# First stage of a convolution and SwiGLU block: low weights on GpSimd, all rows of the conditioning weights on VectorE, tile 0's scale and shift on two engines

## The chip, the cores and the metric

The kernel runs on one core of one Trainium2 chip. A core has TensorE (PE, matrix products into PSUM banks), VectorE (DVE), ScalarE (ACT), GpSimd (POOL), and SyncE (SP), whose queue issues most of the transfers. The metric is the device time of one execution in microseconds (us); lower is better.

## The reference

One layer of a diffusion trunk, with 1024 tokens of 1024 features in fp32. The first stage, which the change touches, computes `h` and the first products of `h @ w_in`:

```python
sh1, sc1, g1, sh2, sc2, g2 = split(silu(c) @ ada_w + ada_b, 6)
h = rmsnorm(x, norm1_g) * (1.0 + sc1) + sh1
gate_b, gate_c, hv = split(h @ conv_w_in, 3)
conv = conv3_grid(gate_c * hv, conv_w)
x = x + g1 * ((gate_b * conv) @ conv_w_out)
x = x + g2 * swiglu(modulate(rmsnorm(x, norm2_g), sh2, sc2), ffn_w_in, ffn_w_out)
out = rmsnorm(x, final_g)
```

## The kernel before

TensorE multiplies in a reduced fp32 format. To keep the precision, each operand is split into a high part (a cast) and a low part (raw minus high), and a product is made of three terms: high x high, low tokens x high weights, high tokens x low weights (TERMS). This holds in all stages. The long later stages (the rest of the convolution mixer by Strassen's scheme, then the SwiGLU) keep TensorE busy and aren't touched.

The first stage has the first 512 tokens and seven column blocks ("pairs", EARLY) of conv_w_in, which fill seven PSUM banks. It goes over the eight feature tiles k = 0 to 7 (128 features each, KD = 8, KH = 4). For each tile it does the following.

- Ada(k) makes tile k's shift and scale: the column sums of ada_w, weighted by silu(c). Its eight "rows" are blocks of 128 input features; each row is a tile of 128 x 256 (shift and scale beside each other). `sums` multiplies rows by their weights into two accumulators (row r goes to accumulator r modulo 2; rows 0 and 1 start them, the others add), `merge` adds the two, `total` sums over the partitions on TensorE, with one-column products in which the accumulators meet a column of ones. A number of rows ("direct") may be left to TensorE, which then multiplies them by the column of weights. `columns` turns the totals into a column of scale1 and one of shift1.
- `tokens(k)` calls `columns`, makes the high tokens (A11h or A12h, from xT, the normalized and transposed tokens) on ScalarE, and has the low weights w0l made (`low0`); `rows_ahead` then sums rows of the next tile.
- `tokens_low(k)` makes the modulated tokens in place (xT), their low part on VectorE (`low1`: A11l, A12l), the cast of the next tile's weights (`high0`: w0h), and the remaining rows of the next tile (`rows_left`, with `merge`).
- The 21 products of a tile go over the pairs term by term (`by_term`); `total_at` says ahead of which of them the next tile's total stands. Tiles 3 and 4 have an order of their own, because the seven banks are copied out half way (`save_p1`, tiles p).

The program's order is the order of the work on SP, DVE, ACT and PE in this stage (a block of manual scheduling); GpSimd's order is set by the scheduler. Loads run ahead by three tiles (`next_loads`). Before tile 0, four token tiles (Tokens) are loaded, normalized (ScalarE squares, GpSimd x_ms and x_r, VectorE scales), transposed by TensorE and copied to xT by ScalarE. `keep_busy` is a filler product on TensorE.

In tile 0 the token tile is modulated twice: A11h on ScalarE, and an unrounded copy h0 (tile h) on VectorE.

Of the kernel before, what the change touches and what calls it, by code (L numbers as in the profile page):

```python
# [11 lines left out]
AF = mybir.ActivationFunctionType  # L12
# [12 lines left out]
def trunk_kernel(ctx: ExitStack, tc: tile.TileContext, x, c, ada_w, ada_b, norm1_g, norm2_g,  # L25
                 conv_w_in, conv_w, conv_w_out, ffn_w_in, ffn_w_out, final_g, out):
    nc = tc.nc
# [18 lines left out]
    def f(ap):  # L46
        return ap.bitcast(F32)
# [16 lines left out]
    def t2(name, shape=None):  # L64
        return sb.tile(shape or [P, H], F32, name=name, tag="t2", bufs=6)
# [7 lines left out]
    def sub(o, a, b):  # L73
        return nc.vector.tensor_tensor(o, a, b, op=ALU.subtract)  # L74
# [67 lines left out]
    class Ada:  # L142
# [26 lines left out]
        def merge(self):  # L169
            add(self.acc[0], self.acc[0], self.acc.pop())  # L170

        def total(self, apart=False):
            self.ps = [bank(f"{self.name}_ps{j}") for j in range(2)] if apart else [ada_ps[0]] * 2
            rows = [(self.rows[r], cs[:, r:r + 1]) for r in range(KD - self.direct, KD)]
            sums = [(acc, ones) for acc in self.acc]
            n = len(rows) + len(sums)
            products = [(j, i, *part) for j in range(2) for i, part in enumerate(rows + sums)]
            if apart:
                products.sort(key=lambda p: p[1] >= len(rows))
            for j, i, part, by in products:  # L180
                nc.tensor.matmul(self.ps[j][:, j:j + 1], lhsT=part[:, j, :], rhs=by, start=i == 0, stop=i == n - 1)  # L181

        def columns(self):

            k = self.k
            nc.scalar.activation(scale1[:, k:k + 1], self.ps[1][:, 1:2], AF.Identity, scale=g1c[:, k:k + 1],
                                 bias=gab1[:, k:k + 1])
            nc.scalar.activation(shift1[:, k:k + 1], self.ps[0][:, 0:1], AF.Identity, bias=ab[:, k:k + 1])

    class AdaRow:  # L190

# [117 lines left out]
    def h_of(k, h):  # L309
        hi, lo = A[QUARTER[h, k // KH], k % KH // 2]  # L310
        return hi[:, k % 2, :], lo[:, k % 2, :]
# [7 lines left out]
            if h == 0:  # L319
                nc.scalar.copy(h_of(k, h)[0], o)  # L320

    def modulate1_both(k, raw=None):

        o, by, plus = xT[0][k // 2][:, k % 2, :], scale1[:, k:k + 1], shift1[:, k:k + 1]
        nc.scalar.activation(h_of(k, 0)[0], o, AF.Identity, scale=by, bias=plus)
        nc.vector.tensor_scalar(o if raw is None else raw, o, by, plus, op0=ALU.mult, op1=ALU.add)

    def low1(k, h):
        hi, lo = h_of(k, h)
        sub(lo, xT[h][k // 2][:, k % 2, :], f(hi))  # L330
# [29 lines left out]
        nc.scalar.copy(w0[k][0], w0raw[k])  # L360

    def low0(k):
        sub(w0[k][1], w0raw[k], f(w0[k][0]))

    def term0(k, pair, terms=range(3)):
        if pair not in xbank:
# [5 lines left out]

    p1_left = []

    def save_p1(pair, tile, later=False):
        nc.scalar.copy(tile, xbank[pair])
        if later:
            p1_left.append((pair, tile))
        else:
            nc.gpsimd.dma_start(aside[PAIRS.index(pair)], tile)  # L380
# [298 lines left out]

    with in_order(ENG.SP, ENG.DVE, ENG.Activation, ENG.PE):  # L680
        xs = [Tokens(t) for t in range(TH)]
        ada = [Ada(0, 2)]
        ada[0].load()
        ada[0].load()
        load0(0)
# [2 lines left out]
        def next_loads(k):  # L688

            if k < KD:  # L690
                ada.append(Ada(k, 2 if k == 1 else 0))
                ada[k].load()
                ada[k].load()
                load0(k)
            elif k == KD:
                xs.extend(Tokens(TH + i) for i in range(TH))
            elif k == KD + 1:
                more.extend(First(pair) for pair in LATER[:2])
                for m in more:
                    m.load(0)  # L700
            elif k == KD + 2:
                more.extend(First(pair) for pair in LATER[2:])
                for m in more[2:]:
                    m.load(0)
                for m in more:
                    m.load(1)
# [6 lines left out]
        for i in range(TH):  # L713
            if i == TH - 1:
                ada[0].sums(0, 1)
            xs[i].scale()
            for g in range(2):
                xs[i].transposes(g)
            xs[i].copies(*(range(KH) if i < TH - 1 else (0,)))
        high0(0)  # L720
        ada[0].sums(2, 3, 4, 5)
        ada[0].total(True)
        keep_busy(1)
        ada[0].columns()
        h0 = t2("h0")
        modulate1_both(0, h0)
        xs[TH - 1].copies(1, 2, 3)
        ada_ps.append(bank("ada_ps"))

        def rows_ahead(k):  # L730

            if k < KD:
                ada[k].sums(2, 3, 4)

        def rows_first(k):
            if k < KD:
                ada[k].sums(0, 1, scalar=True)

        def rows_left(k):
            if k < KD:  # L740
# [24 lines left out]
        def saved(k, n, pair):  # L765
            if k == KH - 1:
                if n % 2 == 0:
                    kept[n // 2] = t_s(f"p1_{n}", [P, 2, H])
                save_p1(pair, kept[n // 2][:, n % 2, :], later=True)

        by_term = [(pair, (i,)) for i in range(3) for pair in EARLY]
        by_half = by_term[:7] + [(pair, (1, 2)) for pair in EARLY]
        first_five, first_four = [[(pair, (i,)) for i in range(3) for pair in EARLY[:n]] +
                                  [(pair, range(3)) for pair in EARLY[n:]] for n in (5, 4)]
        orders = [by_term] * (KH - 1) + [first_five, first_four] + [by_term] * (KH - 2) + [by_half]
        total_at = [14] * (KH - 1) + [11, 12] + [14] * (KH - 1)
        sub(h_of(0, 0)[1], h0, f(h_of(0, 0)[0]))
        rows_first(1)
        tokens(0)
        tokens_low(0)  # L780
        for k in range(KD):
            if k:
                next_loads(k + 3)
            if k + 3 == KD + 2:
                store_p1()
            last = k == KD - 1
            if k == 6:
                nc.vector.tensor_copy(xT[0][0][:, 0, :], h0)
            for n, (pair, terms) in enumerate(orders[k]):
                if n == total_at[k] - 4:  # L790
                    rows_first(k + 2)
                if n == total_at[k] and not last:
                    ada[k + 1].total()
                    tokens(k + 1)
                    if k != KH - 1:
                        tokens_low(k + 1)
                if n == 13 and k == KH - 1:
                    tokens_low(KH)
                term0(k, pair, terms)
                if n == 8 and k == KD - 2:  # L800
                    xs[TH].squares()
                if 2 in terms:
                    saved(k, EARLY.index(pair), pair)
                if last and n > 6:
                    first_done(pair)
                    if n == 7:
                        xs[TH + 1].scale()
                    if n == 9:
                        more[0].weights(0)
                    if n in (8, 10):  # L810
                        xs[TH + 2 + n // 10].squares()
                    if n in (10, 11):
# [681 lines left out]
```

## Time and profile before

| | us |
|---|---|
| median of three runs | 994.28 (994.0, 994.28, 996.03) |
| profiled execution, time | 995.36 |
| its span | 993.6 |
| TensorE busy in the span | 979.7 |
| VectorE, ScalarE, GpSimd busy | 712.8, 490.9, 99.6 |

The span is what the profiler saw between the first and the last instruction; the execution's time has 1.8 us more around it. TensorE's busy time comes from modelled ends of pipelined products, so a wait of a tenth of a microsecond may not show as idle time of PE; the row of its weight loads (PEld) then shows it. In the timeline each row gives the start and the duration in us, the engine, the line, the operation with output and inputs, and, in brackets, the idle time of the engine just before it with what ended it. The one-column products and the filler have two records each.

### The profile page before, as it was taken

The numbers are of one execution on the slowest core, as the hardware profiler recorded it, in microseconds if no ns is written. First come the engines' busy times: TensorE is split into PE (matmuls) and PEld (weight loads), VectorE is DVE, ScalarE is ACT, GpSimd is POOL, SyncE is SP. The second block draws the span as 40 slices with busy tenths as digits, with TensorE's granted clock in tenths as the row PEclk, the third lists the DMA queues.
The fourth block names the chain that finished last, engine by engine and source line by source line (L and its number), as shares of the span: only waits on it lengthen the run. The fifth ranks groups of instructions, "written<-read, shape, count | busy, mean of one in ns | idle before, by whom it ended". The sixth has DMA issues, their size and how long they took to land.

```text
span 993.6 us, 12268 instructions
## 1 busy us (share of the span) xinstructions
PE 979.7 (99%) x4406; PEld 805.7 (81%) x4406; DVE 712.8 (72%) x1015; ACT 490.9 (49%) x789; POOL 99.6 (10%) x176
## 2 busy tenths in 40 slices
PE   8999999999999999999999999999999999999997
PEld 5788888878888878888888888888888888888886
DVE  5868988888656798777765665665665755878885
ACT  7766776675445675244333333333334353534553
POOL 2021001110111200110110110110110110000000
PEclk9999999999999999999999999999999999999999
DMA  9979399996774232535332431431316954577543
GB/s 332 350 266 317 99 277 268 293 284 196 248 229 142 92 106 64 185 133 162 124 117 61 142 117 53 148 117 53 127 53 213 389 185 155 173 265 275 182 144 128
DMA packets 155773, 180.46 MB, mean 182 GB/s; under 512 B 8020, under 2 KB 112576, under 8 KB 155712
## 3 DMA queue, kind: packets, MB, share of 16 engines
q1 hardware_dynamic: 142592, 137.65, 42.8%
q0 software_dynamic: 11888, 38.86, 11.8%
q10 hardware_dynamic: 1232, 3.18, 0.8%
q8 instruction: 34, 0.56, 0.2%
q14 instruction: 27, 0.22, 0.1%
HBM read 135.33 MB, written 38.03 MB: 174 GB/s over the span
## 4 chain that ended last, share of the span: by engine, by line
PE 94%; DVE 2%; DMA 1%; ACT 1%; issue 0%; POOL 0%; SPq 0%; POOLq 0%; DVEq 0%; ACTq 0%
PE X_f L581 24%; PE zP L1422 21%; PE m L471 17%; PE Z_f L581 12%; PE y L1041 7%; PE Y_f L581 6%; PE x L370 3%; PE x L421 3%; DVE BP_f L74 1%; PE x1T L1014 1%; DMA x<-in_x_dram 1%; PE ada_ps L181 0%; PE xT L297 0%; PE zl L1422 0%; DMA vl_t<-vd 0%
## 5 line engine op out<-in xcount | busy, mean ns | idle before, releaser
L74 DVE TENSOR_TENSOR BP_f<-wr_f,BP_f 128x512 fp32r<-128x512 f32 x154 | 105.0, 687 | 61.2 <-ACT BP_f L83 59.5
L83 ACT CAST BP_f<-wr_f 128x512 fp32r<-128x512 f32 x154 | 94.1, 620 | 87.4 <-PE Z_f L581 55.7
L1422 PE MATMUL zP<-w3h_P,a3l_P 128*128 128x512 f32 (+1 forms) x308 | 118.6, 385 | 0.0
L1422 PE MATMUL zP<-w3l_P,a3h_P 128*128 128x512 f32 (+1 forms) x308 | 118.6, 385 | 0.0
L1422 PE MATMUL zP<-w3h_P,a3h_P 128*128 128x512 f32 (+1 forms) x308 | 117.2, 385 | 0.0
L1422 PEld LDWEIGHTS zP<-w3h_P,a3h_P 128*128 128x128 f32 x308 | 57.9, 188 | 11.7
L1422 PEld LDWEIGHTS zP<-w3l_P,a3h_P 128*128 128x128 f32 x308 | 57.9, 188 | 11.6
L1422 PEld LDWEIGHTS zP<-w3h_P,a3l_P 128*128 128x128 f32 x308 | 57.9, 188 | 11.4
L74 DVE TENSOR_TENSOR a3l_P<-a3l_P,a3h_P 128x1024 fp32r<-128x1024 f32 (+1 forms) x42 | 47.4, 1134 | 25.3 <-ACT a3h_P L1266 25.3
L581 PE MATMUL X_f<-A11h,BP_f 128*128 128x512 f32 x176 | 57.7, 390 | 0.0
L581 PE MATMUL X_f<-AS3h,BP_f 128*128 128x512 f32 x176 | 57.7, 389 | 0.0
L581 PE MATMUL X_f<-AS2h,BP_f 128*128 128x512 f32 x176 | 57.6, 389 | 0.0
L581 PE MATMUL X_f<-A22h,BP_f 128*128 128x512 f32 x176 | 57.6, 389 | 0.0
L581 PE MATMUL Z_f<-AS4h,BP_f 128*128 128x512 f32 x176 | 57.6, 389 | 0.0
L581 PE MATMUL Y_f<-A12h,BP_f 128*128 128x512 f32 x176 | 57.5, 389 | 0.0
L581 PE MATMUL Z_f<-AS1h,BP_f 128*128 128x512 f32 x176 | 57.4, 389 | 0.0
L1041 PE MATMUL y<-woh,vh_t 128*128 128x512 f32 x128 | 50.5, 394 | 0.0
L1041 PE MATMUL y<-wol,vh_t 128*128 128x512 f32 x128 | 49.9, 390 | 0.0
L1041 PE MATMUL y<-woh,vl_t 128*128 128x512 f32 x128 | 49.8, 389 | 0.0
L1266 ACT CAST a3h_P<-a3l_P 128x1024 fp32r<-128x1024 f32 (+1 forms) x42 | 40.6, 977 | 14.1 <-DMA a3l_P<-ad_S 7.6
L74 DVE TENSOR_TENSOR wr_f<-wr_f,wr_f 128x512 f32<-128x512 f32 x66 | 45.3, 688 | 1.5
L77 DVE TENSOR_TENSOR u_f<-Z_f,u_f 128x512 f32<-128x512 f32 x22 | 15.2, 691 | 37.3 <-ACT u_f L598 34.7
(318 smaller groups left out, 2339.6 us busy)
## 6 DMA issues: line engine op xcount, KB each, us to landing
wr_f<-in_ffn_w_in_dram SPq DMA_DIRECT2D x44, 512.0 KB, 3.8
ada_w<-in_ada_w_dram SPq DMA_DIRECT2D x64, 256.0 KB, 5.6
w_P<-in_ffn_w_out_dram SPq DMA_DIRECT2D x30, 512.0 KB, 4.9
a3l_P<-ad_S SPq DMA_DIRECT2D x20, 512.0 KB, 5.8
ad<-a POOLq DMA_DIRECT2D x33, 256.0 KB, 2.5
ada_w<-in_ada_w_dram SPq DMA_DIRECT2D x16, 512.0 KB, 5.5
a3l_P<-ad SPq DMA_DIRECT2D x15, 512.0 KB, 4.1
wr<-in_conv_w_in_dram SPq DMA_DIRECT2D x12, 512.0 KB, 7.5
```

Source lines behind the costliest of these rows:

```text
L74: return nc.vector.tensor_tensor(o, a, b, op=ALU.subtract)
L77: return nc.vector.tensor_tensor(o, a, b, op=ALU.add)
L83: nc.scalar.copy(hi, raw)
L370: nc.tensor.matmul(xbank[pair], lhsT=w0[k][wi][:, place[pair], :], rhs=h_of(k, 0)[hi], start=(k == 0 and i == 0), stop=(k == KD - 1 and i ...
L421: nc.tensor.matmul(xbank[self.pair], lhsT=self.w[wi][:, k, :], rhs=h_of(half * KH + k, 0)[hi], start=(half == 0 and k == 0 and i == 0), st ...
L471: nc.tensor.matmul(self.ps[a], lhsT=self.w[pname][wi][:, k, a * P:(a + 1) * P], rhs=A[aname, k // 2][hi][:, k % 2, :], start=(q == 0 and k ...
L581: mm = nc.tensor.matmul(ps, lhsT=w[:, wi, 2 * kp + kk, :], rhs=A[aname, kp][hi][:, kk, :], start=(first and kp == 0 and kk == 0 and i == 0 ...
L1014: nc.tensor.transpose(ps2[:, i * P:(i + 1) * P], xn[:, k * P:(k + 1) * P], ident)
L1041: mm = nc.tensor.matmul(ys[t][n], lhsT=vt[t][vi][:, k, :], rhs=wo[k][wi][:, n * H:(n + 1) * H], start=(k == 0 and i == 0), stop=(k == KD - ...
L1266: nc.scalar.copy(hi, f(lo))
L1422: mm = nc.tensor.matmul((zs[t] if to is None else to)[:, cols], lhsT=a[ai][:, k % 2, t * P:(t + 1) * P], rhs=w[wi][:, k % 2, cols], start= ...
```

## The change

Five things change in the first stage.

- `low0` goes from VectorE to GpSimd, for all eight tiles.
- Rows 0 and 1 of tiles 1 to 7 go from ScalarE (`rows_first`, four products ahead of a total) to VectorE, at the head of `rows_ahead`. VectorE thus sums all eight rows of these tiles, five ahead of the low tokens and three behind. Tile 1 leaves no rows to TensorE any more (it left two).
- Tile 0 leaves three rows to TensorE instead of two, whose products now stand ahead of the transposes of the fourth token tile; its two accumulators are merged on VectorE ahead of the total.
- Tile 0's scale stays on ScalarE, its shift becomes an addition on VectorE. h0 goes from VectorE to ScalarE, behind A11h. The rows of tile 1 are in part summed ahead of tile 0's low tokens, and its total stands two products later (16).
- Of the seven copies of banks half way, two (n = 2 and 4) go from ScalarE to VectorE.

```diff
-            self.ps = [bank(f"{self.name}_ps{j}") for j in range(2)] if apart else [ada_ps[0]] * 2   # in total(apart)
+        def banks(self, apart=False): self.ps = ...                                                  # the same
+        def total(self, which=("rows", "sums")):      # the same products, bank by bank, of the kinds in which
         def columns(self):
-            nc.scalar.activation(shift1[:, k:k + 1], self.ps[0][:, 0:1], AF.Identity, bias=ab[:, k:k + 1])
+            if k:
+                nc.scalar.activation(shift1[:, k:k + 1], self.ps[0][:, 0:1], AF.Identity, bias=ab[:, k:k + 1])
+            else:
+                add(shift1[:, :1], self.ps[0][:, 0:1], ab[:, :1])
...
     def low0(k):
-        sub(w0[k][1], w0raw[k], f(w0[k][0]))
+        nc.gpsimd.tensor_tensor(w0[k][1], w0raw[k], f(w0[k][0]), op=ALU.subtract)
...
-    def save_p1(pair, tile, later=False):
-        nc.scalar.copy(tile, xbank[pair])
+    def save_p1(pair, tile, later=False, vector=False):
+        (nc.vector.tensor_copy if vector else nc.scalar.copy)(tile, xbank[pair])
...
-        ada = [Ada(0, 2)]
+        ada = [Ada(0, 3)]
-                ada.append(Ada(k, 2 if k == 1 else 0))
+                ada.append(Ada(k))
...
             if i == TH - 1:
                 ada[0].sums(0, 1)
+                ada[0].banks(apart=True)
+                ada[0].total(("rows",))
             xs[i].scale()
...
         high0(0)
-        ada[0].sums(2, 3, 4, 5)
-        ada[0].total(True)
+        ada[0].sums(*range(2, KD - ada[0].direct))
+        ada[0].merge()
+        ada[0].total(("sums",))
         keep_busy(1)
         ada[0].columns()
+        nc.scalar.activation(h_of(0, 0)[0], xT[0][0][:, 0, :], AF.Identity, scale=scale1[:, :1], bias=shift1[:, :1])
         h0 = t2("h0")
-        modulate1_both(0, h0)
+        nc.scalar.activation(h0, xT[0][0][:, 0, :], AF.Identity, scale=scale1[:, :1], bias=shift1[:, :1])
         xs[TH - 1].copies(1, 2, 3)
+        ada[1].sums(0, 1, 2)
...
         def rows_ahead(k):
-                ada[k].sums(2, 3, 4)
-        def rows_first(k):
-                ada[k].sums(0, 1, scalar=True)
+                ada[k].sums(*range(5))
...
-                save_p1(pair, kept[n // 2][:, n % 2, :], later=True)
+                save_p1(pair, kept[n // 2][:, n % 2, :], later=True, vector=n in (2, 4))
...
-        total_at = [14] * (KH - 1) + [11, 12] + [14] * (KH - 1)
+        total_at = [16] + [14] * (KH - 2) + [11, 12] + [14] * (KH - 1)
         sub(h_of(0, 0)[1], h0, f(h_of(0, 0)[0]))
-        rows_first(1)
-        tokens(0)
-        tokens_low(0)
+        low0(0)
+        high0(1)
+        ada[1].sums(*range(3, KD - ada[1].direct))
+        ada[1].merge()
...
-                if n == total_at[k] - 4:
-                    rows_first(k + 2)
                 if n == total_at[k] and not last:
+                    ada[k + 1].banks()
                     ada[k + 1].total()
```

TensorE at the start of the stage, before: the transposes of the third and fourth token tile (xT), tile 0's column sums (ada_ps), the filler (idle_ps), the first product (x).

```order
L297 MATMUL xT_1_238<-ident,x_137 128x128 x4
L297 MATMUL xT_0_250<-ident,x_139 128x128 x4
L297 MATMUL xT_1_255<-ident,x_139 128x128 x4
L181 MATMUL ada_ps_268<-cols,ada_w_146 128x1 x2
L181 MATMUL ada_ps_269<-cols,ada_w_146 128x1 x2
L181 MATMUL ada_ps_268<-ones,ada_acc_141 128x1
L181 MATMUL ada_ps_268<-ones,ada_acc_142 128x1
L181 MATMUL ada_ps_269<-ones,ada_acc_141 128x1
L181 MATMUL ada_ps_269<-ones,ada_acc_142 128x1
L121 MATMUL idle_ps<-idle,ident 128x512
L370 MATMUL x_2_300<-A11h_118,w0h_261 128x512
```

The same place after:

```order
L302 MATMUL xT_1_238<-ident,x_137 128x128 x4
L182 MATMUL ada_ps_249<-cols,ada_w_146 128x1 x3
L182 MATMUL ada_ps_250<-cols,ada_w_146 128x1 x3
L302 MATMUL xT_0_258<-ident,x_139 128x128 x4
L302 MATMUL xT_1_263<-ident,x_139 128x128 x4
L182 MATMUL ada_ps_249<-ones,ada_acc_141 128x1
L182 MATMUL ada_ps_250<-ones,ada_acc_141 128x1
L121 MATMUL idle_ps<-idle,ident 128x512
L369 MATMUL x_2_302<-A11h_118,w0h_269 128x512
```

The products with rows of ada_w moved ahead of the last eight transposes and grew from four to six; those with accumulators fell from four to two.

VectorE in tile 1, before, from the low tokens of tile 1 to those of tile 2 (ada_acc ahead of w0l: tile 2's rows, behind it tile 3's; w0l: low weights of tile 2):

```order
L74 TENSOR_TENSOR A11l_119<-xT_0_110,A11h_118 128x512
L167 SCALAR_TENSOR_TENSOR ada_acc_164<-ada_w_168,cols,ada_acc_164 128x256
L167 SCALAR_TENSOR_TENSOR ada_acc_163<-ada_w_168,cols,ada_acc_163 128x256
L167 SCALAR_TENSOR_TENSOR ada_acc_164<-ada_w_168,cols,ada_acc_164 128x256
L77 TENSOR_TENSOR ada_acc_163<-ada_acc_163,ada_acc_164 128x256
L74 TENSOR_TENSOR w0l_339<-w0r_171,w0h_338 128x896
L167 SCALAR_TENSOR_TENSOR ada_acc_352<-ada_w_354,cols,ada_acc_352 128x256
L167 SCALAR_TENSOR_TENSOR ada_acc_353<-ada_w_354,cols,ada_acc_353 128x256
L167 SCALAR_TENSOR_TENSOR ada_acc_352<-ada_w_357,cols,ada_acc_352 128x256
L74 TENSOR_TENSOR A11l_123<-xT_1_111,A11h_122 128x512
```

The same place after:

```order
L74 TENSOR_TENSOR A11l_119<-xT_0_110,A11h_118 128x512
L167 SCALAR_TENSOR_TENSOR ada_acc_164<-ada_w_168,cols,ada_acc_164 128x256
L167 SCALAR_TENSOR_TENSOR ada_acc_163<-ada_w_168,cols,ada_acc_163 128x256
L167 SCALAR_TENSOR_TENSOR ada_acc_164<-ada_w_168,cols,ada_acc_164 128x256
L77 TENSOR_TENSOR ada_acc_163<-ada_acc_163,ada_acc_164 128x256
L165 TENSOR_SCALAR ada_acc_350<-ada_w_352,cols 128x256
L165 TENSOR_SCALAR ada_acc_351<-ada_w_352,cols 128x256
L167 SCALAR_TENSOR_TENSOR ada_acc_350<-ada_w_352,cols,ada_acc_350 128x256
L167 SCALAR_TENSOR_TENSOR ada_acc_351<-ada_w_352,cols,ada_acc_351 128x256
L167 SCALAR_TENSOR_TENSOR ada_acc_350<-ada_w_355,cols,ada_acc_350 128x256
L74 TENSOR_TENSOR A11l_123<-xT_1_111,A11h_122 128x512
```

The low weights are gone and two row products came; what stands between the low tokens and the merge is the same.

ScalarE between tiles 3 and 4, before, from tile 4's scale on (p: copies of banks):

```order
L186 ACTIVATE scale_106<-ada_ps,gab_89,cols 128x1
L188 ACTIVATE shift_107<-ada_ps,cols 128x1
L748 ACTIVATE A12h_120<-xT_2_112,shift_107,scale_106 128x512
L376 COPY p_0_491<-x_1_302 128x512
L376 COPY p_2_505<-x_2_304 128x512
L757 ACTIVATE xT_2_112<-xT_2_112,shift_107,scale_106 128x512
L376 COPY p_2_505<-x_1_306 128x512
L376 COPY p_4_516<-x_0_308 128x512
```

The same place after:

```order
L188 ACTIVATE scale_106<-ada_ps,gab_89,cols 128x1
L191 ACTIVATE shift_107<-ada_ps,cols 128x1
L747 ACTIVATE A12h_120<-xT_2_112,shift_107,scale_106 128x512
L375 COPY p_0_487<-x_1_304 128x512
L756 ACTIVATE xT_2_112<-xT_2_112,shift_107,scale_106 128x512
L375 COPY p_2_503<-x_1_308 128x512
L375 COPY p_4_514<-x_2_312 128x512
```

One copy ahead of xT and one behind it went to VectorE, where the first stands just ahead of tile 4's low tokens and the second behind the merge of tile 5's rows. On GpSimd the eight low parts stand one behind the other between the x_r of the fourth token tile and the x_ms of the fifth; each waits for its raw weights and their cast.

More of the change, by code (lines that the diff above doesn't have):

```diff
@@ L170, in merge, with banks @@
             add(self.acc[0], self.acc[0], self.acc.pop())
-        def total(self, apart=False):
+        def banks(self, apart=False):
             self.ps = [bank(f"{self.name}_ps{j}") for j in range(2)] if apart else [ada_ps[0]] * 2
[L174 to L181, printed above, removed]
+        def total(self, which=("rows", "sums")):
+            parts = [("rows", self.rows[r], cs[:, r:r + 1]) for r in range(KD - self.direct, KD)]
+            parts += [("sums", acc, ones) for acc in self.acc]
+            for j in range(2):
+                for i, (kind, part, by) in enumerate(parts):
+                    if kind in which:
+                        nc.tensor.matmul(self.ps[j][:, j:j + 1], lhsT=part[:, j, :], rhs=by, start=i == 0,
+                                         stop=i == len(parts) - 1)
         def columns(self):
@@ L320, in modulate1 @@
                 nc.scalar.copy(h_of(k, h)[0], o)
[L322 to L326, printed above, removed]
     def low1(k, h):
@@ L732, in rows_ahead @@
             if k < KD:
-                ada[k].sums(2, 3, 4)
-        def rows_first(k):
-            if k < KD:
-                ada[k].sums(0, 1, scalar=True)
+                ada[k].sums(*range(5))
         def rows_left(k):
```

## The prediction

> **What bounds the kernel now.** I read the page first (engines and slices), then the granted clock in stretches of 1 us, then the timeline of the first stage, because the change touches nothing behind it.
>
> ```profile
> PE 979.7 (99%) x4406; PEld 805.7 (81%) x4406; DVE 712.8 (72%) x1015; ACT 490.9 (49%) x789; POOL 99.6 (10%) x176
> PE   8999999999999999999999999999999999999997
> ```
>
> TensorE is busy in 99% of the span and only the first slice is loose. So time can come from two places: when TensorE starts the first stage, and the fractions of a microsecond in which that stage waits. Whatever is won there moves all that follows.
>
> The start, in the timeline (start, duration, engine, line, idle before in brackets):
>
> ```profile
> 10.37 1.09 PE L297 MATMUL xT<-ident,x 128*128 128x128 f32 x8 [0.37 <-DVE x L291]
> 11.86 1.66 DVE L167 SCALAR_TENSOR_TENSOR ada_acc<-ada_w,cols,ada_acc 128x256 f32<-128x256 f32 x4
> 12.08 1.06 PE L297 MATMUL xT<-ident,x 128*128 128x128 f32 x8 [0.62 <-DVE x L291]
> 12.98 0.95 PE L181 MATMUL ada_ps<-cols,ada_w 128*128 128x1 f32 x8
> 13.01 0.99 ACT L360 CAST w0h<-w0r 128x896 fp32r<-128x896 f32 x1
> 13.79 1.03 PE L181 MATMUL ada_ps<-ones,ada_acc 128*128 128x1 f32 x8
> 14.86 0.35 ACT L186 ACTIVATE scale<-ada_ps,gab,cols 128x1 f32<-128x1 f32 x1 [0.86 <-PE ada_ps L181]
> 15.12 0.25 ACT L188 ACTIVATE shift<-ada_ps,cols 128x1 f32<-128x1 f32 x1
> 15.40 0.81 ACT L325 ACTIVATE A11h<-xT,shift,scale 128x512 fp32r<-128x512 f32 x1
> 16.27 2.77 PE L370 MATMUL x<-A11h,w0h 128*128 128x512 f32 x7
> 21.53 0.36 PE L181 MATMUL ada_ps<-ones,ada_acc 128*128 128x1 f32 x2
> 22.47 0.82 ACT L748 ACTIVATE A11h<-xT,shift,scale 128x512 fp32r<-128x512 f32 x1
> 23.47 1.78 PE L370 MATMUL x<-A11h,w0h 128*128 128x512 f32 x7
> ```
>
> The first product of tile 0 (16.27) stands behind column sums, scale, shift and the modulated tokens. Its seven products take 2.77 us, those of tile 1 take 1.78: the granted clock was half. The rows are one stretch each (us; PE, PEld, DVE, ACT, POOL busy; clock; DMA):
>
> ```profile
> 14.00:15.00 1.00, 1.00 (x9) 1.00 (x9) 0.00 (x0) 0.14 (x2) 0.00 (x0) 0.90 1.15 355
> 18.00:19.00 1.00, 1.00 (x5) 0.77 (x5) 1.00 (x3) 1.00 (x3) 0.00 (x0) 0.89 1.15 347
> ```
>
> The dip runs from 14.8 (0.90 = a fifth of the stretch at half) to 18.2.
>
> From tile 1 on, a tile is a ring of engines:
>
> ```profile
> 24.04 0.93 ACT L360 CAST w0h<-w0r 128x896 fp32r<-128x896 f32 x1
> 24.16 0.69 DVE L74 TENSOR_TENSOR A11l<-xT,A11h 128x512 fp32r<-128x512 f32 x1 [1.99 <-ACT xT L757]
> 24.77 1.27 DVE L167 SCALAR_TENSOR_TENSOR ada_acc<-ada_w,cols,ada_acc 128x256 f32<-128x256 f32 x3
> 26.08 0.43 DVE L77 TENSOR_TENSOR ada_acc<-ada_acc,ada_acc 128x256 f32<-128x256 f32 x1
> 26.42 1.08 DVE L74 TENSOR_TENSOR w0l<-w0r,w0h 128x896 fp32r<-128x896 f32 x1
> 26.70 0.50 PE L181 MATMUL ada_ps<-ones,ada_acc 128*128 128x1 f32 x4
> 27.06 1.86 PE L370 MATMUL x<-A11h,w0l 128*128 128x512 f32 x7
> 28.64 1.47 PEld L370 LDWEIGHTS x<-A11h,w0h 128*128 128x128 f32 x7 [0.15 <-ACT A11h L748]
> 29.47 0.69 DVE L74 TENSOR_TENSOR A11l<-xT,A11h 128x512 fp32r<-128x512 f32 x1 [0.78 <-ACT xT L757]
> ```
>
> Low part of the tokens, three rows, merge, total on TensorE, scale, next tokens: from 24.16 to 29.47 is 5.31 us, and TensorE waits 0.15 of it for the tokens. TensorE and the ring are nearly level; what lengthens the ring lengthens the tile.
>
> **The change, part by part.**
>
> *Start of tile 0.* Six row products (three rows, two banks) now stand ahead of the last transposes, instead of four behind them. Eight records (four products, two records each) take 12.98 to 13.79, 0.20 us a product, so six take 1.2. They can start when the transposes of token tile 2 end, 10.37 + 1.09 = 11.46; their data is there by then (the last of these loads, issued at 5.8, landed 5.6 us later, at 11.4):
>
> ```profile
> L156 SPq DMA_DIRECT2D ada_w<-in_ada_w_dram x1: 368/368/368, 5.8 to 5.8; - x1
> DMA to landing us min/median/max: 5.6/5.6/5.6
> ```
>
> So the last transposes move from 12.08 to about 12.7, 0.6 later, and behind them on ScalarE the copy of the first bank and the cast at 13.01 move by as much less a slack of 0.05: the cast ends at 14.56. On the other path VectorE has three sums and a merge in place of four sums (1.25 + 0.43: done at 13.5), TensorE two products instead of four (13.8 to 14.2), so the total is there at 14.2 and the cast is what ends last. Scale (0.35) then ends at 14.95; shift is an addition on VectorE beside it, under 0.43 us by the row of the merge; the tokens start at 14.97 instead of 15.40: 0.43 earlier. The unrounded copy h0 now follows on ScalarE (0.81) instead of running on VectorE beside; the low tokens are thus made at 16.6 to 17.3 instead of from 16.25, still ahead of the second seven products (18.88 before). No cost.
>
> *Tile 0 to tile 1.* TensorE starts at 15.84. At half clock a product takes 0.46 us (16.27 to 18.88 for seven), at full 0.23. To 18.2 go 5.1 products, the other 10.9 of the sixteen ahead of the total end at 20.7. VectorE has merged by 17.3 + 5 x 0.42 + 0.43 = 19.8, so nothing waits. The total is two products instead of six (tile 1 no longer leaves two rows to TensorE): 0.36, at 21.06. From the total's end (21.53 + 0.36 = 21.89) to the first product of tile 1 (23.47) went 1.58 us; the five products left take 1.15, so this chain decides and TensorE waits 0.4. Tile 1 starts at 22.64 instead of 23.47: **-0.8 us**. Ends: if the dip goes, sixteen products end at 19.5, the merge at 19.8 decides, tile 1 starts at 21.75: -1.7; if the row products push the cast further, -0.4. I take -0.8, because the row of the dip is what this run shows.
>
> *Work that moves and nobody waits for.* ScalarE loses two row products a tile, VectorE a low part and gains two row products:
>
> ```profile
> L163 ACT ACTIVATE ada_acc<-ada_w,cols 128x256 f32<-128x256 f32 x14 | 6.4, 511 | 0.0
> L165 DVE TENSOR_SCALAR ada_acc<-ada_w,cols 128x256 f32<-128x256 f32 x2 | 0.7, 340 | 0.0
> ```
>
> ScalarE 2 x 0.51 less, VectorE 1.08 - 0.68 = 0.40 less, in the part of the ring where VectorE waits 0.78 for xT anyway (29.47): zero. If that cover went, 0.40 would show as a gain.
>
> *Middle of the stage, tile 4.* Two of seven bank copies go from ScalarE to VectorE.
>
> ```profile
> 39.06 1.05 ACT L376 COPY p<-x 128x512 f32<-128x512 f32 x2
> 40.01 0.82 ACT L757 ACTIVATE xT<-xT,shift,scale 128x512 f32<-128x512 f32 x1
> 40.72 2.04 ACT L376 COPY p<-x 128x512 f32<-128x512 f32 x4
> 41.35 0.19 PEld L370 LDWEIGHTS x<-A12h,w0h 128*128 128x128 f32 x1 [0.93 <-ACT p L376]
> ```
>
> One copy less ahead of xT (1.05 / 2 = 0.5) brings xT, the copy behind it and so the product at 41.35 forward by that; VectorE's first copy lies in its wait for xT, the second behind the merge, where TensorE first does the total. **-0.45**, ends 0 and -0.93 (the whole wait).
>
> *The low weights on GpSimd.* Each starts when the cast is done, 24.04 + 0.93 = 24.97 in the ring above, which is in the middle of the three rows and the merge that decide. It is read 0.1 us behind the total of the next tile (27.06 plus a tile, 32.4), so it has over 7 us. Do the two engines disturb each other?
>
> ```profile
> 53.96 0.43 DVE L77 TENSOR_TENSOR ada_acc<-ada_acc,ada_acc 128x256 f32<-128x256 f32 x1
> 53.98 0.46 POOL L260 TENSOR_SCALAR x_ms<-x_ss 128x1 f32<-128x1 f32 x1 [42.98 <-ACT x_sq L287]
> 811.57 1.22 DVE L74 TENSOR_TENSOR w3l_P<-w_T,w3h_P 128x1024 fp32r<-128x1024 f32 x1 [1.91 <-PE zP L1422]
> 811.70 3.74 POOL L1447 TENSOR_SCALAR fg<-fg 128x1024 f32<-128x1024 f32 x1 [31.84 <-PE zP L1422]
> 813.40 1.37 DVE L74 TENSOR_TENSOR a3l_P<-a3l_P,a3h_P 128x1024 fp32r<-128x1024 f32 x1 [0.61 <-ACT a3h_P L1266]
> L74 DVE TENSOR_TENSOR a3l_P<-a3l_P,a3h_P 128x1024 fp32r<-128x1024 f32 x12 | 14.6, 1220 | 9.5 <-ACT a3h_P L1266 9.5
> ```
>
> Yes, unevenly. GpSimd's one-element operation ends 0.05 us after VectorE's merge does, so it waited for it. The large one at 811.70 took 3.74 us, with VectorE in two-input operations for 1.09 + 1.37 of it; 1.28 remain for 1024 elements. VectorE's operation that began in the middle of it took 1.37 against 1.22, +0.15. For a low part of 896 elements with two inputs this gives 1.1 us (as one input) to 2.2 (twice that) free of VectorE; in the open 3.3 to 6.5. I take 2.2, since the work has two inputs. [...]
>
> What VectorE pays: three starts lie behind 24.97 in the ring (two rows, the merge). At +0.15 a start this is 0.45 a tile; in proportion to length (12% of 1.27) 0.15. I take 0.3, the middle. It counts in five rings (those in which tiles 2, 3, 4, 6 and 7 get their scales; in tile 0 the merge has 0.9 us to spare, tile 5's low part starts behind its merge): **+1.5**, ends 0 and +2.25; a gain is excluded, since nothing on VectorE gets shorter there.
>
> *Queues.* On GpSimd the eight low parts stand ahead of the sums x_ms of the second token half (53.98); the last of them begins one ring earlier than tile 7 and has until VectorE has made tile 7's low tokens, behind which the scaling stands that reads these sums. On SP's queue the later loads of raw weights now wait for GpSimd, where they waited for VectorE; the tiles that they fill are read much later. Zero, with 0 and +0.5 as ends.
>
> **Sum.** -0.8 - 0.45 + 1.5 = +0.25. The profiled execution took 995.36 us (span 993.6), the median of the three runs 994.28; on the median that is 994.5. A measurement of this kernel can tell about 0.2%, 2 us, from no change; +0.25 is inside. Its own range: -1.7 - 0.93 = -2.6 to -0.4 + 2.25 + 0.5 = +2.35, 991.7 to 996.6.
>
> **Rivals.**
> *Faster.* The half clock does not come (the filler product now begins inside the stretch ahead of the dip), and VectorE is hardly disturbed: -1.7 - 0.45 + 0.1 = -2.05, 992.2. For it: 1.37 against 1.22 is little. Against it: that stretch holds more one-column products than before, not fewer. It decides below 0.05 us a ring.
> *GpSimd starves (slower).* It was held off by VectorE in every row above. In the ring VectorE is idle about 5.31 - 2.35 (24.16 to 26.51) - 0.68 - 1.27 = 1.0 us a tile. If only that is free, a low part of 2.2 us needs more than two tiles; the tile must grow until 2.2 are idle, +1.2 for five tiles, +6, in all +4.75: 999.0. Against it: behind the merge at 53.96 GpSimd came through although VectorE went on. It decides from the point where a low part needs more than 1.0 plus what slips in between operations.
> *VectorE is locked out (slower).* Behind the row at 24.77 GpSimd gets in and keeps VectorE off for all of its 2.2 us: +2.2 in five rings, +11, in all +9.75: 1004.0. The row at 813.40 speaks against it (+0.15, not +2). [...]
>
> **How the numbers follow.** Forecast 0.50, faster 0.25, starved 0.16, locked 0.09. Of the forecast 0.03 lies beyond +2 us, so faster than 992.3: 0.25; within: 0.47; slower than 996.3: 0.28. The predicted time is the forecast's, 994.5. The range 991.6 to 999.5 leaves out a part of the faster case (0.06), the upper part of the starved one (0.04) and the locked one (0.09).
>
> **What would show it.** First product of tile 0 near 15.8, of tile 1 near 22.6; TensorE's wait at tile 4's fourth product near 0.4; low parts on POOL of 2.2 to 5 us each; rows and merge of a ring longer than 1.27 and 0.43 by 0.3 together, starts of tiles 5.6 apart. Rows of unchanged length or no half clock speak for the faster rival; weight loads of w0l that wait for POOL for the starved one; a gap of 2 us in VectorE's rows for the locked one. The prediction is wrong if VectorE's price per ring is not near 0.3.

## The result, and the profile after

| | before | after |
|---|---|---|
| median of the runs made side by side (4 and 4), us | 994.5 | 1006.49 |
| lowest to highest, us | 994.0 to 996.03 | 1006.27 to 1006.8 |
| profiled execution, its span, us | 995.36, 993.6 | 1006.52, 1004.7 |

The change makes the kernel slower: 1.0113 times the time before, 95% interval 1.0101 to 1.0125, or 12 us. Forecast was 994.5, with a range from 991.6 to 999.5.

The page's engines and slices after:

```profile
span 1004.7 us, 12244 instructions
PE 985.5 (98%) x4398; PEld 809.0 (81%) x4398; DVE 723.5 (72%) x1025; ACT 485.5 (48%) x773; POOL 115.7 (12%) x184
PE   7899999999999999999999999999999999999996
```

Shares tell nothing here. VectorE's busy time rose by 10.7 us although its low weights are gone, which is the first hint: an instruction that stands still counts as busy. The timeline of the ring in which tile 2 gets its scale shows it (start, duration, engine, line; the same place as the ring shown of before):

```profile
23.83 0.35 ACT L188 ACTIVATE scale<-ada_ps,gab,cols 128x1 f32<-128x1 f32 x1 [4.67 <-PE ada_ps L182]
25.93 0.93 ACT L359 CAST w0h<-w0r 128x896 fp32r<-128x896 f32 x1
26.06 0.69 DVE L74 TENSOR_TENSOR A11l<-xT,A11h 128x512 fp32r<-128x512 f32 x1 [1.28 <-ACT xT L756]
26.67 3.12 DVE L167 SCALAR_TENSOR_TENSOR ada_acc<-ada_w,cols,ada_acc 128x256 f32<-128x256 f32 x3
26.94 2.17 POOL L362 TENSOR_TENSOR w0l<-w0r,w0h 128x896 fp32r<-128x896 f32 x1 [5.40 <-DMA ada_w<-in_ada_w_dram]
29.82 0.42 DVE L77 TENSOR_TENSOR ada_acc<-ada_acc,ada_acc 128x256 f32<-128x256 f32 x1
30.30 0.61 PE L182 MATMUL ada_ps<-ones,ada_acc 128*128 128x1 f32 x4 [0.21 <-DVE ada_acc L77]
30.95 0.35 ACT L188 ACTIVATE scale<-ada_ps,gab,cols 128x1 f32<-128x1 f32 x1 [4.09 <-PE ada_ps L182]
```

The three rows took 1.27 us before and take 3.12 now, 1.85 more. One row of them has it all. Shortest, median and longest of the four rows between 26 and 31 us, in ns:

```profile
L167 DVE SCALAR_TENSOR_TENSOR ada_acc<-ada_w,cols,ada_acc x4: 470/478/2328, 26.7 to 30.7; 128x256 f32<-128x256 f32 x4
```

GpSimd's low part begins at 26.94, while the first of the three rows runs, and ends at 29.11. The second row, the first to begin beside it (27.07), lasts 2.33 us, to 29.39; the others keep their 0.48. GpSimd hardly waited for VectorE (2.17 us, 2.12 beside an idle VectorE in e8), VectorE stood still for GpSimd (2.33 instead of 0.48). Rows, merge, total and scale all move: the two scales are 7.12 us apart (23.83 to 30.95), 5.31 before.

What waits for what in the first 110 us (total, times, longest). After, ScalarE's scale waits for the total, and the total for the merge:

```profile
ACT scale L188 <- PE ada_ps L182: 22.2, 7, 4.7
PE ada_ps L182 <- DVE ada_acc L77: 6.1, 5, 2.1
```

Before, the scale waited less than half as long:

```profile
ACT scale L186 <- PE ada_ps L181: 9.1, 6, 2.5
```

The rings, worked out from the starts of ScalarE's eight scales in the timelines and of the next stage's first product (us from one tile's scale to the next tile's; e1 to e8 are experiments below):

| ring | before | after | e1 | e2 | e5 | e8 |
|---|---|---|---|---|---|---|
| tile 0's scale at | 14.86 | 15.62 | 14.86 | 14.91 | 15.39 | 14.07 |
| 0 to 1 | 7.07 | 8.21 | 6.84 | 7.65 | 6.14 | 6.76 |
| 1 to 2 | 5.31 | 7.12 | 5.28 | 7.13 | 5.33 | 5.76 |
| 2 to 3 | 5.29 | 7.13 | 5.29 | 7.14 | 5.31 | 5.84 |
| 3 to 4 | 5.28 | 7.12 | 5.28 | 7.12 | 5.28 | 5.83 |
| 4 to 5 | 6.46 | 5.81 | 5.81 | 6.47 | 6.46 | 6.63 |
| 5 to 6 | 5.54 | 7.61 | 5.71 | 7.48 | 5.56 | 6.13 |
| 6 to 7 | 5.27 | 7.20 | 5.27 | 7.20 | 5.32 | 5.83 |
| 7 to next stage | 8.14 | 8.15 | 8.14 | 8.16 | 8.23 | 8.17 |

The five rings to tiles 2, 3, 4, 6 and 7 give +9.5 of the +10.75 by which the next stage begins later; the start of tile 0 gives 0.76, the ring behind it 1.14, tile 4's ring -0.65. The other 0.4 of the span's 11.1 lies behind the first stage; there the kept executions differ by 0.6 among themselves.

### The profile page after: what moved, and what is told of

It reads as the page before. It is cut to its first block, busy times and chain, and to the rows that moved or that the text cites. A ratio compares the mean times of both kernels' runs of the same rounds, so it can differ in the third digit from the quotient of the medians.

```text
span 1004.7 us, 12244 instructions
## 1 busy us (share of the span) xinstructions
PE 985.5 (98%) x4398; PEld 809.0 (81%) x4398; DVE 723.5 (72%) x1025; ACT 485.5 (48%) x773; POOL 115.7 (12%) x184
## 4 chain that ended last, share of the span: by engine, by line
PE 90%; DVE 3%; issue 2%; DMA 2%; SPq 1%; POOL 1%; ACT 1%; POOLq 0%; ACTq 0%; DVEq 0%
PE X_f L580 23%; PE zP L1421 20%; PE m L470 16%; PE Z_f L580 12%; PE y L1040 7%; PE Y_f L580 6%; PE x L420 3%; DVE ada_acc L167 1%; DMA wf<-in_conv_w_in_dram 1%; PE x L369 1%; POOL w0l L362 1%; DVE BP_f L74 1%; PE x1T L1013 1%; SPq L156 1%; SPq L353 0%
```

## The experiments

Each ratio is to the kernel before, run side by side, with its 95% interval.

**One edit undone, and done alone.** e1 is the changed kernel with the low weights back on VectorE; e2 is the kernel before with nothing but them on GpSimd.

```diff
 e1, on the changed kernel:
-        nc.gpsimd.tensor_tensor(w0[k][1], w0raw[k], f(w0[k][0]), op=ALU.subtract)
+        sub(w0[k][1], w0raw[k], f(w0[k][0]))
 e2, on the kernel before:
-        sub(w0[k][1], w0raw[k], f(w0[k][0]))
+        nc.gpsimd.tensor_tensor(w0[k][1], w0raw[k], f(w0[k][0]), op=ALU.subtract)
```

> The changed kernel with one thing undone: the low parts of the weights are made on VectorE again, everything else as changed. Theory 'shut out' (GpSimd's two-input operation keeps VectorE off the memory for its whole 2.2 us): the three rows of a ring are back at 1.27 us instead of 3.12, rings at 5.3 to 5.5 us, the time at 994 to 996. Rival 'VectorE overloaded' (the two added rows and the moved start cost the time): rings stay near 7.1 and the time at 1004 or more.

> The kernel before with one thing done: the low parts of the weights on GpSimd, nothing else. Shut out: five rings of 7.1 instead of 5.3 us, about 1003 to 1005. VectorE overloaded: VectorE has less to do than before, so 994 to 995.

e1: 995.34 us, 0.9996 (0.9986 to 1.0005). e2: 1006.41, 1.0112 (1.0096 to 1.0129). The one line carries the whole loss; all other parts together make no difference that can be told. For e2, 1003 to 1005 had been expected from five longer rings; a sixth, 0 to 1, is longer too (7.65 against 7.07). The groups of VectorE's row sums, of after and of e1 (count, then busy time and mean of one):

```profile
L167 DVE SCALAR_TENSOR_TENSOR ada_acc<-ada_w,cols,ada_acc 128x256 f32<-128x256 f32 x45 | 30.2, 724 | 0.0
```

```profile
L167 DVE SCALAR_TENSOR_TENSOR ada_acc<-ada_w,cols,ada_acc 128x256 f32<-128x256 f32 x45 | 19.1, 480 | 0.0
```

The same 45 instructions cost 11.1 us more. In e2 the ring reads like that of after:

```profile
25.39 3.13 DVE L167 SCALAR_TENSOR_TENSOR ada_acc<-ada_w,cols,ada_acc 128x256 f32<-128x256 f32 x3
25.66 2.19 POOL L363 TENSOR_TENSOR w0l<-w0r,w0h 128x896 fp32r<-128x896 f32 x1 [4.53 <-DMA ada_w<-in_ada_w_dram]
```

**What in GpSimd's operation does it.** e3 splits each low part into seven of 128 x 128. e4 gives GpSimd one input of the same size instead of two; it leaves the third term out (the low weights become zeros).

```diff
 e3, on the changed kernel:
+        for i in range(7):
+            nc.gpsimd.tensor_tensor(w0[k][1][:, i, :], w0raw[k][:, i, :], f(w0[k][0])[:, i, :], op=ALU.subtract)
 e4, on the changed kernel:
+        nc.gpsimd.tensor_scalar(w0[k][1], w0raw[k], 0.0, None, op0=ALU.mult)
```

> The changed kernel with each low part made by seven GpSimd operations of 128x128 instead of one of 128x896. Shut out for the length of one instruction: VectorE gets in between the pieces, each of its three operations behind the cast waits for one piece of about 0.35 us, rings +0.9 instead of +1.85, about 1001 to 1002. Shut out until GpSimd has no more work: the rows stay at 3.1 us or longer, 1006 to 1008.

> The changed kernel with the low part replaced by a GpSimd operation of the same size with one input (raw weights times zero), so the third term of the first stage's products is left out in effect. If what counts is that GpSimd reads and writes the memory, VectorE is shut out for its whole length, some 1.0 to 1.3 us: rings +0.6 to +0.9, about 1000 to 1002. If one-input operations let VectorE in, as the 1.37 us against 1.22 of the kernel before suggested: rings +0.15 to +0.45, 995 to 998.

e3: 999.03, 1.0035 (1.0024 to 1.0046). Its timeline:

```profile
24.64 1.69 DVE L167 SCALAR_TENSOR_TENSOR ada_acc<-ada_w,cols,ada_acc 128x256 f32<-128x256 f32 x3
24.91 3.87 POOL L363 TENSOR_TENSOR w0l<-w0r,w0h 128x128 fp32r<-128x128 f32 x7 [2.03 <-ACT w0h L359]
26.36 0.57 DVE L77 TENSOR_TENSOR ada_acc<-ada_acc,ada_acc 128x256 f32<-128x256 f32 x1
```

Between pieces VectorE gets its turn: three rows take 1.69 (+0.42), the merge 0.57 (+0.14), each operation 0.14 more on the mean. The rings to tiles 2 to 4 are 5.82 and 5.83 long, and GpSimd pays with 3.87 instead of 2.2. So what hurts is how long one GpSimd operation keeps VectorE out, not that GpSimd works. The time is better than the 1001 to 1002 that the theory had given, which had put a piece at 0.35 us for each of VectorE's operations. That 0.14 is close to the +0.15 a start of the prediction is chance: that figure came from one large operation.

e4: 996.38, 1.0011 (1.0002 to 1.002), inside the 995 to 998 of the second theory. GpSimd's operation no longer reads the cast and so begins at other places; in two rings it met VectorE as follows:

```profile
26.41 1.94 DVE L167 SCALAR_TENSOR_TENSOR ada_acc<-ada_w,cols,ada_acc 128x256 f32<-128x256 f32 x3
26.43 2.78 POOL L362 TENSOR_SCALAR w0l<-w0r 128x896 fp32r<-128x896 f32 x1 [2.57 <-DMA w0r<-in_conv_w_in_dram]
30.60 2.59 POOL L362 TENSOR_SCALAR w0l<-w0r 128x896 fp32r<-128x896 f32 x1 [1.39 <-DMA w0r<-in_conv_w_in_dram]
30.84 1.04 DVE L77 TENSOR_TENSOR ada_acc<-ada_acc,ada_acc 128x256 f32<-128x256 f32 x1
```

Rows 1.94 instead of 1.27 (+0.67), merge 1.04 instead of 0.43 (+0.61), while GpSimd's operation lasts 2.6 to 2.8 us. In each of e4's eight low parts one VectorE instruction is longer, by 0.5 to 0.8 us (in tile 0's a second one, by 0.4); the others keep their usual length although GpSimd's operation goes on. A one-input operation holds VectorE off for a fifth to a third of its time in the other seven, a two-input one for nearly all of it (1.85 of 2.17). GpSimd's spans are rough in this profile, so the shares are less sure than VectorE's own lengths. Since e4 also moved where the two meet, its time alone proves nothing of this; the rows do. Whether the number of inputs or the kind of operation decides, e4 doesn't tell apart.

**Where it falls.** e5 is e2 with each low part held on GpSimd until the merge of its own tile is done, by a one-element operation that reads the merged accumulator (and GpSimd's order in this stage is the program's). e8 does the same to the changed kernel.

```diff
 e5 and e8, ahead of low0(k):
+            if k:
+                nc.gpsimd.tensor_scalar(tiny(f"after{k}"), ada[k].acc[0][:, 0, :1], 1.0, EPS, op0=ALU.mult, op1=ALU.add)
             low0(k)
```

> The kernel before with the low parts of the weights on GpSimd (one operation of 128x896 each), but each held back until VectorE has done the merge of the ring (a one-element GpSimd operation that reads the merged sum stands ahead of it). Shut out, as a sum of works: GpSimd's 2.2 us now fall on the three rows that VectorE does ahead, which have 1.9 us of slack with the low part gone, so the low tokens come 0.3 to 0.5 late: rings 5.6 to 5.8, about 997 to 998. If the price were paid for any GpSimd work wherever it falls, rings stay at 7.1 and the time at 1004 to 1006; if only the collision with rows and merge counted, rings 5.3 and 995.

> The changed kernel, with each low part (tiles 1 to 7) held on GpSimd until the merge of its own tile's rows is done, by a one-element GpSimd operation that reads the merged accumulator. Theory A (the shut-out is 1.87 us wherever it falls, and all that VectorE does between one tile's low tokens and the next is one chain): 0.69 + 1.27 + 0.43 + the two new row products 0.68 + three rows 1.27 + 1.87 = 6.2 us a ring instead of 5.3, so 0.9 in some six rings: 999 to 1000.5 us, with the row products (now behind the merge) as the rows that are long. Theory B (only a collision with the three rows ahead of the merge costs anything): rings of 5.3, 994.5 to 996 us. Theory C (the order of GpSimd's work is not what costs, the number of its operations is): rings of 7.1 as in the changed kernel, 1006 us.

e5: 995.32, 0.9999 (0.999 to 1.0008). Its timeline:

```profile
24.38 1.27 DVE L167 SCALAR_TENSOR_TENSOR ada_acc<-ada_w,cols,ada_acc 128x256 f32<-128x256 f32 x3
25.68 0.42 DVE L77 TENSOR_TENSOR ada_acc<-ada_acc,ada_acc 128x256 f32<-128x256 f32 x1
26.02 3.14 DVE L167 SCALAR_TENSOR_TENSOR ada_acc<-ada_w,cols,ada_acc 128x256 f32<-128x256 f32 x3
26.63 2.25 POOL L363 TENSOR_TENSOR w0l<-w0r,w0h 128x896 fp32r<-128x896 f32 x1
29.09 0.69 DVE L74 TENSOR_TENSOR A11l<-xT,A11h 128x512 fp32r<-128x512 f32 x1
```

VectorE is kept out for 1.87 us as before (3.14 against 1.27), but behind the merge, where nobody waits: the low weights that stood there are gone (1.08) and so is the wait for xT (0.78), together 1.86. The low tokens begin with no wait shown ahead of them, and the rings to tiles 2, 3, 4 and 7 are 5.28 to 5.33. The same collision costs 11 us in one place and nothing in the other (expected for the sum of works: 997 to 998; for a price of rows and merge alone: 995).

e8: 998.55, 1.0033 (1.0021 to 1.0045). There VectorE also sums the two rows that ScalarE had, and the slack is spent:

```profile
25.81 0.61 DVE L165 TENSOR_SCALAR ada_acc<-ada_w,cols 128x256 f32<-128x256 f32 x2
26.28 2.12 POOL L362 TENSOR_TENSOR w0l<-w0r,w0h 128x896 fp32r<-128x896 f32 x1
26.34 3.14 DVE L167 SCALAR_TENSOR_TENSOR ada_acc<-ada_w,cols,ada_acc 128x256 f32<-128x256 f32 x3
29.40 0.68 DVE L74 TENSOR_TENSOR A11l<-xT,A11h 128x512 fp32r<-128x512 f32 x1
```

The rings to tiles 2, 3, 4 and 7 are 5.76 to 5.84, 0.5 more than before; VectorE's rows stand back to back, and it is now the engine that sets the ring. Theory A was right in kind, though 998.55 lies just below its 999 to 1000.5. Its 6.2 was too much: it added durations that overlap at their edges (the low tokens last 0.68, but the next operation starts 0.61 after them), and 5.83 is the sum from start to start. The place alone (theory B, at most 996) does not make it free.

**The other parts, and a better version.** e6 has, on the kernel before, two copies of banks on VectorE, one more row ahead, and tile 0's shift on VectorE. e7 is e1 with six rows ahead and two behind, tile 1's total at 14 and tile 0's low weights behind the merge. e9 is e7 with the other totals two products earlier.

```diff
 e7, on e1:
-                ada[k].sums(*range(5))
+                ada[k].sums(*range(6))
-                ada[k].sums(*range(5, KD - ada[k].direct))
+                ada[k].sums(*range(6, KD - ada[k].direct))
-        total_at = [16] + [14] * (KH - 2) + [11, 12] + [14] * (KH - 1)
+        total_at = [14] * (KH - 1) + [11, 12] + [14] * (KH - 1)
-        low0(0)                    # now behind ada[1].merge()
 e9, on e7:
+        total_at = [14] + [12] * (KH - 2) + [11, 12] + [12] * (KH - 1)
 e6, on the kernel before:
-                save_p1(pair, kept[n // 2][:, n % 2, :], later=True)
+                save_p1(pair, kept[n // 2][:, n % 2, :], later=True, vector=n in (2, 4))
```

> A try at a better version, from the kernel before, nothing on GpSimd: one more row ahead of the low tokens (four ahead, two behind), two bank copies and tile 0's shift on VectorE. If the ring of engines sets the tile, it falls from 5.30 to TensorE's own 5.15 us in five rings (-0.7), tile 4 gives -0.6 and the start -0.2: ratio about 0.9985. If TensorE's own work sets it already, only the latter two: 0.999.

> A try at a better version, from the changed kernel with the low parts on VectorE: one more row ahead of the low tokens, tile 1's total two products earlier, and tile 0's low part behind the merge of tile 1's rows. Against that kernel tile 1 starts about 0.5 us earlier, and rings fall by 0.1, since VectorE then has 5.2 us of work in each; against the kernel before -1.5 us, ratio about 0.9985. If VectorE's work fills the ring, the rings stay at 5.3: 0.999.

> The version with the low parts on VectorE, six rows ahead and two behind (e7), with the totals two products earlier (12 instead of 14). Theory A (with the ring on VectorE short of 5.3, the total's place sets the tile: 14 products, 1.58 us from total to tokens): the chain loses two products of 0.23, the ring becomes what VectorE and 21 products (4.9 with loads) allow: 0.1 to 0.2 less in five rings, 993.3 to 994 us. Theory B (the merge is not ready two products earlier, TensorE waits for it): 994.3 us or later, with waits of the total for the merge in every ring.

e6: 994.3, 0.9992 (0.9983 to 1.0001): tile 4's ring fell from 6.46 to 5.82, which is too little to tell in the time; of the five rings that were to fall to 5.15 only that from tile 3 to 4 did. e7: 994.26, 0.9988 (0.9979 to 0.9997), faster than before by about 1.2 us, but not told apart from e6 or e9. e9: 994.45, 0.999 (0.9981 to 0.9999): no gain over e7 in the time, where 993.3 to 994 had been hoped for. In e7 the ring 0 to 1 fell to 5.83 (6.84 in e1), and the next gave 0.99 back (6.27 against 5.28 in e1). The weight loads of TensorE say why:

```profile
20.78 1.46 PEld L369 LDWEIGHTS x<-A11h,w0l 128*128 128x128 f32 x7 [0.42 <-DVE w0l L74]
24.49 1.46 PEld L369 LDWEIGHTS x<-A11l,w0h 128*128 128x128 f32 x7 [0.66 <-DVE A11l L74]
```

The scale comes early, but VectorE's low weights and low tokens are late in its place. In e9 TensorE's weight loads stand end to end from 27.36 on but for 0.46 at tile 4's copies, and the rings behind the first two are 5.20 to 5.27 long (5.83 with these copies): 21 products and a total fill them. The way from tile 7 to the next stage then takes 8.58 instead of 8.14, and about half of the 0.94 that the rings won over e7 is gone. In e9's profiled execution tile 0 also came 1.18 later than in e7's (15.83 against 14.65), with the slow transposes of which more below. Little more is to be had from this ring.

## Why the prediction was wrong

*The low weights on GpSimd (+1.5): the step that failed.* Its places were right but for one: five rings, to tiles 2, 3, 4, 6 and 7, and none to tile 5; a sixth, to tile 1, paid too (below). Its price was not: 1.8 to 2.1 a ring instead of 0.3, +9.5 instead of +1.5. It was taken from a row that did not show this case, in two ways. First, at 813.40 GpSimd had one input; here it has two, and e4 shows that the form of GpSimd's operation (one input or two, with the operation that goes with it) changes what VectorE pays from 0.65 to 1.85. I had scaled GpSimd's own time for the second input but not VectorE's price. No row of before has a large two-input operation of GpSimd beside VectorE, so the upper end had to be a full stop of VectorE, and the range should have reached it.

Second, +0.15 was not the price of a one-input operation either. The same GpSimd operation stands in every run, and in seven of them (after, e1, e3, e4, e5, e8, e9) it begins just ahead of VectorE's. In after:

```profile
822.06 2.81 POOL L1446 TENSOR_SCALAR fg<-fg 128x1024 f32<-128x1024 f32 x1 [31.48 <-DMA fg<-in_final_g_dram]
822.29 1.89 DVE L74 TENSOR_TENSOR w3l_P<-w_T,w3h_P 128x1024 fp32r<-128x1024 f32 x1 [1.91 <-PE zP L1421]
824.13 1.23 DVE L74 TENSOR_TENSOR a3l_P<-a3l_P,a3h_P 128x1024 fp32r<-128x1024 f32 x1
```

VectorE's first subtraction takes 1.83 to 2.08 in these seven instead of 1.22, 0.6 to 0.9 more, and GpSimd's start lies 0.9 us ahead of the end of this extra time in each of them. In before (and e2, e6, e7) VectorE came first: GpSimd's operation took 3.74 to 3.85 instead of 2.8, and VectorE then stood idle for 0.6 us. The idle 0.61 and the 0.15 of the row at 813.40 together lie inside 0.6 to 0.9: most of the price fell into idle time, and the row showed the end of it.

The length of the low part, 2.2 us, came out right (2.12 alone, 2.23 on the mean), but by luck: it was put at twice 1.1 for one input, and e4's one-input operations took 2.45 to 2.90.

*The rival "VectorE is locked out"* had the course, the size and the place: 2.2 in five rings, 1004.0; measured were 1.85 in the rows, and 1006.49. I gave it 0.09 because one row, misread as above, spoke against it. It missed on the low side because of tile 0: by the next tile the profile is 1.9 us late (0.76 + 1.14), where the sum had -0.8. Part of this is the start, of which more below; the larger part is the merge, for which I had counted 0.9 us of slack. There tile 1's low part meets five rows:

```profile
18.70 3.91 DVE L167 SCALAR_TENSOR_TENSOR ada_acc<-ada_w,cols,ada_acc 128x256 f32<-128x256 f32 x5
23.21 0.58 PE L182 MATMUL ada_ps<-ones,ada_acc 128*128 128x1 f32 x4 [2.05 <-DVE ada_acc L77]
```

3.91 against 2.07 in e1, and the total waits 2.05 for the merge: the ring is 8.21 against 6.84 of e1, a sixth one that pays (+1.37).

The runs show the order and the lengths. With the two-input low part VectorE is out for nearly all of GpSimd's operation (26.94, 2.17: out for 1.85); with e4's one-input operations it waits too, but not as long (2.6 to 2.8 us: out for 0.6 to 0.7). What it is that VectorE waits for, no run here shows. In the ring from 23.83 the first of the three rows, begun at 26.67 and so before the low part, kept its 0.48; the second, begun beside it, did not. At 50.03 after shows both sides again:

```profile
50.03 0.68 DVE L375 COPY p<-x 128x512 f32<-128x512 f32 x1
50.11 2.11 POOL L362 TENSOR_TENSOR w0l<-w0r,w0h 128x896 fp32r<-128x896 f32 x1 [6.75 <-DVE ada_acc L77]
50.63 2.00 DVE L165 TENSOR_SCALAR ada_acc<-ada_w,cols 128x256 f32<-128x256 f32 x2
```

The copy out of a bank, begun 0.08 us ahead of GpSimd, takes its 0.68 (as at 46.13, with GpSimd idle); the two row products behind it, which have one full-size input each, take 2.00 instead of 0.61. Whether a copy begun beside GpSimd would be held up as well, no run tests.

*The rival "GpSimd starves"* fell: the eight low parts take 2.23 us each on the mean, nearly as if alone (2.12, the last one of e8, at 56.92, beside an idle VectorE). In the ring shown above GpSimd got in at 26.94, although VectorE's operations stand back to back from 26.06 to 30.24.

```profile
L362 POOL TENSOR_TENSOR w0l<-w0r,w0h 128x896 fp32r<-128x896 f32 x8 | 17.8, 2227 | 34.9 <-ACT w0h L359 22.8 <-DVE ada_acc L77 6.7 <-DMA ada_w<-in_ada_w_dram 5.4
```

*Start of tile 0 (-0.43).* From the scaling of the fourth token tile to the first product: before 16.27 - 11.20 = 5.07, e1 16.11 - 11.71 = 4.40, e8 15.33 - 10.93 = 4.40. So the step holds, with 0.67, where the transposes ahead run as usual. In the profile of after they didn't:

```profile
8.75 3.99 PE L302 MATMUL xT<-ident,x 128*128 128x128 f32 x24
12.58 1.40 PE L182 MATMUL ada_ps<-cols,ada_w 128*128 128x1 f32 x12
16.87 1.88 PE L369 MATMUL x<-A11h,w0h 128*128 128x512 f32 x7 [0.66 <-ACT A11h L727]
```

```profile
10.89 1.09 PE L302 MATMUL xT<-ident,x 128*128 128x128 f32 x8 [0.92 <-DVE x L296]
11.82 1.40 PE L182 MATMUL ada_ps<-cols,ada_w 128*128 128x1 f32 x12
14.02 0.94 ACT L359 CAST w0h<-w0r 128x896 fp32r<-128x896 f32 x1
16.11 1.88 PE L369 MATMUL x<-A11h,w0h 128*128 128x512 f32 x7 [0.39 <-ACT A11h L727]
```

After needs 3.99 us for 24 transposes with no wait between them, e1 1.09 for the last eight of them; the products with rows of ada_w, predicted at 11.46, begin at 12.58 and 11.82. Why the transposes of that execution were slow is open; the granted clock there is 1.00. The low weights on GpSimd don't explain it: e9, which has them on VectorE, took 4.45 us for the same 24 in its profiled execution, and e3, with them on GpSimd, did not show it. So the 0.76 of tile 0's start belongs to one execution, and not surely to the change.

*Tile 0 to tile 1 (-0.8).* The half clock that I counted on did not come (seven products in 1.88, where they took 2.77), but the -1.7 for that case did not either. In e1 the merge starts at 20.51, not at 19.4, since the low weights of tile 0 stand ahead of the rows on VectorE again, and the total waits 1.05 for it: ring 6.84 against 7.07, -0.23. In after the collision above ate all of it; tile 0's merge was the term that the sum had put at nothing.

*Middle, tile 4 (-0.45).* Right. The wait of the weight load for the bank went from 0.93 to 0.47 (I had 0.4), and the ring from 6.46 to 5.81; in e1, where nothing else disturbs, the ring behind it gave 0.17 back, so -0.48 stayed. The line is of after:

```profile
48.27 0.19 PEld L369 LDWEIGHTS x<-A12h,w0h 128*128 128x128 f32 x1 [0.47 <-ACT p L375]
```

*Work that moves and nobody waits for (0), queues (0).* Right: e1's rings to tiles 2, 3, 4 and 7 are 5.27 to 5.29 where before had 5.27 to 5.31, and the ring from tile 7 to the next stage is 8.15 against 8.14.

## What to carry to other kernels

Work given to an idle GpSimd is not free because GpSimd is idle: look at which of VectorE's instructions will run while it does (here one of three rows paid 1.85 of GpSimd's 2.17 us), and price the collision at the whole length of the GpSimd operation until a row with the same operation and the same number of inputs shows less. Such a row counts only if VectorE was not idle while GpSimd began; otherwise part of the price is hidden in the idle time (0.61 us in before). If the collision can't be avoided, put it where VectorE has slack (here behind the merge, 11 us against nothing), or cut the GpSimd operation into pieces so that VectorE gets its turn between them (e3, seven pieces: 999.03 against 1006.49).

## What the runs showed of the hardware

- The profile counts an instruction that is shut out as busy, so no wait appears on VectorE; the sign is the mean of its group (480 ns to 724).
- GpSimd's subtraction takes 2.1 to 2.4 us for 128 x 896 (2.12 alone). Seven pieces of 128 x 128 beside a working VectorE take 3.87, 0.55 each.
- Its one-input operation of 128 x 1024 takes 2.8 us, and VectorE's two-input subtraction begun beside it 1.83 to 2.08 instead of 1.22, in seven executions, as if held off for the first 0.9 of GpSimd's.
- VectorE's one-input scaling of 128 x 1024 takes 0.74 us (11.20 of before), its two-input subtraction of that size 1.22.
- In three of the long rings of after the half clock came back (0.50 from 25 to 28, from 39 to 41 and from 59 to 62), without a price of its own. The stretches of 1 us (PE, PEld, DVE, ACT, POOL busy; clock; DMA) in two of these and, at 36, in a ring that stayed at the full clock:

```profile
25.00:26.00 1.00, 0.84 (x3) 0.67 (x3) 0.00 (x0) 0.97 (x3) 0.00 (x0) 0.50 1.14 347
36.00:37.00 1.00, 0.00 (x0) 0.00 (x0) 0.97 (x3) 0.00 (x0) 0.24 (x1) 1.00 1.15 345
39.00:40.00 1.00, 1.00 (x3) 0.79 (x3) 0.24 (x1) 0.97 (x2) 0.00 (x0) 0.50 1.07 310
```

The ring from 30.95 to 38.08 ran at the full clock, with TensorE idle for the whole stretch at 36, and took 7.13 us; those from 23.83 and from 38.08 had over 3 us at half clock and took 7.12. Either way the ring was as long as VectorE's work made it.
